# One step of a hybrid decoder layer on one core: the sample's queries are stored eight times for the spread loads, and the planned order comes from another list

## The chip, the cores and the metric

The kernel runs on one core of one Trainium2 chip. The metric is the device time of one execution in microseconds; less is better. A core has five instruction queues, one for each engine: TensorE (PE, matmuls and transposes), VectorE (DVE), ScalarE (ACT), GpSimd (POOL) and SyncE (SP), which in this kernel issues every DMA. Each engine runs its queue in order, and engines wait for each other by semaphores. Sixteen DMA engines do the transfers.

## What is computed

One step of one layer for a prompt of 2048 tokens and for a sample of 8 sequences with 8 new tokens each. Every token row is normed and projected, then goes through two mixers: dilated sliding-window attention with 8 heads of 64, and gated linear attention (GLA) with 4 heads. Both are gated and projected back. In outline, from the reference:

```
h = rmsnorm(x, norm_w)
z = h @ w_in
q, k, v, qb, kb, vb, g_lr, gate_a, gate_b = split(z)
q = rope(rmsnorm(heads(q, 8), q_norm_w), pos)
k = rope(rmsnorm(heads(k, 8), k_norm_w), pos)
o_a = mixture over (window, dilation) in ((128, 1), (512, 4), (2048, 16)) of softmax attention
o_b = rmsnorm(gla_chunked(qb / 8, kb, vb, log_sigmoid(g_lr @ w_gate_up + b_gate) / 16, s0))
y = x + concat(o_a * silu(gate_a), o_b * silu(gate_b)) @ w_out
```

For the sample, the keys and values of the last 2048 positions come from a cache in HBM, and each new token attends to 129 cached or new positions in each of the three branches.

## The kernel before

The prompt has 16 tiles of 128 tokens; the sample is one tile of 64 rows, the tile "s". Weights are split into two f16 parts, activations too, so that a projection of a prompt tile to 512 columns is 24 matmuls (L1748). In the order of time the kernel projects v, q and k of all tiles, runs the attention of branches 1 and 2 beside it (`unit`, with `attend`), then branch 3 beside the projections for GLA, then GLA, the gate of mixer B (`gb`), and last the output projection (L2111, `finish`), beside which the rest of the sample's attention is done.

The sample's attention against the cache is in two parts. For branches 2 and 3 each query needs its own set of 128 cached keys, so no matmul is used. `sample_scores(b, t)` handles the token t of sequence b, 64 calls in all: it loads the query's row, 512 f32 numbers, into all 128 partitions (tile `qb`, L1613, called the spread load here), loads 128 keys of the dilation 16 (`k3`, L1615), for t below 4 also 128 keys of the dilation 4 (`k2`, L1618), multiplies on POOL (`dot`, L1603) and sums over the head's 64 columns on DVE (L1604) into `sck`. After the eight tokens of a sequence `sck` goes to `sc_d` in HBM. The tiles `qb` and `k3` have two buffers each, `k2` and the product `pr` have one. `sample_pair` reads `sc_d` much later (`Sc`), beside the output projection.

The queries come from `q_d`, a scratch array in HBM. Before, it has 2048 + 64 rows of 512, of which the last 64 are written and read: `qk_store` writes the sample's tile with one DMA (L1425), the 64 spread loads read a row each, and `sample_new` reads all 64 rows once more in the last stage (L2257).

Ahead of the output projection stand, for each tile, the gate (`so_gb`, `sa_gb` and `gw`, L1297 to L1389), the mix of the three branches (`combine`, L2141 to L2166: weights `w` from the branch's denominators, three products `tc`, their sum, and `mix`), its two f16 parts (`mt`, L2066 and L2067) and their transposes (`tm`, L2076). The output weights are scaled and split on ACT and DVE (`w_o`, L1278 and L1279).

The order of the instructions is not that of the program. The class `Plan` reads the traced program, gives each instruction a cost and each DMA a cost of the queue and a delay of landing (`price`), and lists which instructions depend on which. `settle` then runs a planner (`order`, a list scheduler with one queue for each engine and one for all DMAs, and `backward`) for some rounds to get a priority for each instruction, moves the priorities by a list of steps, and runs `order` once more; `fix` makes the outcome the order of each engine. In `price`, a load whose source's first step is 0 (one row to all partitions) has 3.16 times the cost that its bytes would have, other loads in short rows 1.11 times. Before, a step is a seed: `moved` draws from it an instruction, a kind of group (the instructions that write the same tile; the one instruction; those of its engine within a reach) and an amount.

Of the kernel before, what the change touches and what calls it, by code (L numbers as in the profile page):

```python
# [18 lines left out]
P = 128  # L19
# [4 lines left out]
S = 2048  # L24
NT = S // P
NS = 64
EPS = 1e-6
BIG = 3.0e38
LEVELS = [1, 2, 4, 8, 16, 32, 64]
# [22 lines left out]
class Plan:  # L52
# [581 lines left out]
                released(x)  # L634
        return place

    def moved(self, seed):

        import random

        r = random.Random(seed)
        n, kind = r.randrange(self.real), r.random()
        by = r.gauss(0, 1) * r.choice((1e3, 3e3, 1e4, 3e4))
        if kind < 0.5:
            return self.mates[self.leaf[n]], by
        if kind < 0.6:
            return [n], by
        reach, own = r.choice((1e4, 3e4, 1e5)), self.stem[n]
        return [
            x for x in range(self.real)  # L650
            if self.eng[x] == self.eng[n] and abs(self.base[x] - self.base[n]) < reach
            and (kind > 0.85 or self.stem[x] == own)
        ], by

    def settle(self, rounds, land, traffic, cross, bias, steps):

        self.rank()
        self.lands = {n: x + land for n, x in self.lands.items()}
        self.late = [
            x * (traffic if self.eng[n] == "SP" else 1.0) for n, x in enumerate(self.late)  # L660
        ]
        self.cross = cross
        prio = [-f for f in self.rank()]
        for _ in range(rounds):
            self.order(prio, bias)
            prio = [-x for x in self.backward(self.start)]
        self.leaf = [next((t for t, w, m in reversed(a) if w), "?") for a in self.acc]
        self.stem = [t.rstrip("_0123456789") for t in self.leaf]
        self.mates, self.base = {}, list(prio)
        for n, t in enumerate(self.leaf):  # L670
            self.mates.setdefault(t, []).append(n)
        for seed in steps:
            some, by = self.moved(seed)
            for x in some:
                prio[x] += by
        return self.order(prio, bias)[1]

# [13 lines left out]
def tile_hymba(ctx: ExitStack, tc: tile.TileContext, A: dict):  # L691
    nc = tc.nc
    PE, ACT, DVE, POOL, SP = nc.tensor, nc.scalar, nc.vector, nc.gpsimd, nc.sync
# [5 lines left out]
    def scratch(name, rows, cols):  # L699
        return dram.tile([rows, cols], F32, name=name)  # L700

    RT = S + NS
    q_d = scratch("q_d", RT, 512)
    k_d = scratch("k_d", RT, 512)
    v_d = scratch("v_d", RT, 512)
    zqk_d = scratch("zqk_d", RT, 512)
# [8 lines left out]
    sc_d = scratch("sc_d", 8 * P, 128)  # L715
    oa_d = scratch("oa_d", 2 * NS, 256)
    h_d = dram.tile([NT * P, 2 * KT * P], F16, name="h_d")
# [251 lines left out]
    with ExitStack() as c1:  # L969
# [114 lines left out]
        def fetch(t):  # L1084
            n = NS if t == "s" else P
            if t in (0, 1, 2, 3):
# [332 lines left out]
        def qk_store(nm_, o, n, t, rows):  # L1419
            if nm_ == "k":  # L1420
                SP.dma_start(kn_s if t == "s" else kw_p[rows, :], o[:n])
            if t == "s":
                if nm_ == "q":
                    ACT.activation(o[:n], o[:n], AF.Copy, scale=unq[:n])
                SP.dma_start((q_d if nm_ == "q" else k_d)[rows, :], o[:n])  # L1425
                return
            p_ = xp.tile([P, NH, 2, HD], F16, name=f"{nm_}p_{t}", tag=f"{nm_}p", bufs=1)
            src = o.rearrange("p (h d) -> p h d", h=NH)
            h, l = p_[:, :, 0], p_[:, :, 1]
            if nm_ == "k":  # L1430
                ACT.activation(h, src, AF.Copy, scale=scl["k"][:])
                DVE.scalar_tensor_tensor(l, src, scl["k"][:], h, ALU.mult, ALU.subtract)
            else:
                ACT.activation(h, src, AF.Copy)
                DVE.tensor_tensor(l, src, h, ALU.subtract)
            SP.dma_start(
                (qp_d if nm_ == "q" else kp_d)[rows, :], p_[:].rearrange("p h a d -> p (h a d)")
            )
# [156 lines left out]
            ]  # L1595


        q_s = q_d[S : S + NS, :]
        sk_state = {}

        def dot(out, kt, qt, tag):
# [6 lines left out]
        def sample_scores(b, t):  # L1608
# [1 line left out]
                sk_state["sc"] = sk.tile([P, 2, 64], F32, name=f"sck_{b}", tag="sc")  # L1610
            sc = sk_state["sc"]
            qt = sk.tile([P, 512], F32, name=f"qb_{b}_{t}", tag="qbc")
            SP.dma_start(qt[:], q_s[8 * b + t : 8 * b + t + 1, :].to_broadcast([P, 512]))  # L1613
            k3 = sk.tile([P, 512], F32, name=f"k3_{b}_{t}", tag="k3")
            SP.dma_start(k3[:], ck[b].rearrange("(m r) c -> r m c", r=16)[t])  # L1615
            if t < 4:
# [258 lines left out]
        for i in range(3):  # L1875
            for lst, nm_ in ((st["qbd"], "qbd"), (Sbd, "Sbd"))[: 2 if i < 2 else 1]:
                t = gst.tile([P, 2, 256], F32, name=f"{nm_}{i}")
# [350 lines left out]
        for nh in range(2):  # L2228
            t = cb1.tile([P, NT + 1], F32, name=f"inv_o{nh}")
# [22 lines left out]
        QUADS = [(u, bb) for u in range(2) for bb in range(2)]  # L2252

        def sample_new():
            for nm_, src in (("q", q_d), ("k", k_d)):
                x = ssk.tile([NS, 512], F32, name=f"ls_{nm_}", tag="k1")
                SP.dma_start(x[:], src[S : S + NS, :])  # L2257
                pt = ps_P.tile([P, 512], F32, name=f"ts_{nm_}", tag="PT")
                for p in range(4):
                    PE.transpose(  # L2260
# [160 lines left out]
        weave(out, [sample_attention(), 4 * 9])  # L2421

    steps = (
# [33 lines left out]
    )  # L2457
    plan = Plan(tc, nc)
    plan.fix(plan.settle(7, 600.0, 1.15, 60.0, 10.0, steps))


# [92 lines left out]
```

## Time and profile before

| what | value |
|---|---|
| three runs | 1267.63, 1264.02, 1263.77 us; median 1264.02 |
| the profiled execution | 1262.71 us |
| its span, first to last instruction | 1260.9 us |
| mean granted TensorE clock | 0.994 |
| DMA packets, bytes | 235832, 283.08 MB, mean 225 GB/s |

The profile is one execution taken by the hardware profiler. Its page has the busy time of each engine, the same in 40 slices, the chain of work that ended last, and the costliest groups of instructions. The trace behind it can be asked for stretches of time, waits, single tiles and instructions in order of time. In a row of a stretch stand its length, the busy time of each engine with the number of instructions, the granted TensorE clock, the busy share of the 16 DMA engines, and the rate. In a row of a wait stand who waited, for whom, the total, how often, and the longest. In a row of the order of time stand start, length, engine, line, operation, tiles, and in brackets how long the engine had been idle. A row of a tile's view has the least, the median and the longest duration in ns, and the first and the last start.

### The profile page before, as it was taken

To read this page: it belongs to the slowest core of one execution; us is meant where nothing else is said; L and a number is where in the kernel's file an instruction comes from. 1 tells how busy PE (TensorE), PEld (TensorE's weight loads), DVE (VectorE), ACT (ScalarE), POOL (GpSimd) and SP (SyncE) were. 2 spreads that over 40 slices of the span, in tenths; PEclk is the share of its full clock that TensorE was granted. 3 is DMA by queue.
4 is the path that set the end of the run, shared out by engine and by line. 5 is a ranking of instruction groups with operands and counts; after the bars stand their busy time and mean duration, and the time that the engine had idled before them with its cause. 6 is when DMAs were issued, how large, how long until landed. Compare 5 with 4: busy or idle time off the path is not lost.

```text
span 1260.9 us, 26211 instructions
## 1 busy us (share of the span) xinstructions
PE 1202.4 (95%) x8942; PEld 723.7 (57%) x8942; DVE 956.1 (76%) x2450; ACT 817.8 (65%) x2191; POOL 549.0 (44%) x475
## 2 busy tenths in 40 slices
PE   5999999999999999998999999999999969999998
PEld 2444465667566566766677656665666435445443
DVE  7987887999889777777877557788888795269562
ACT  6654697889599888968778424678878632123220
POOL 0155433665755244643444766646533162024230
PEclk9999999999999999999999999999999979999999
DMA  8579935876945898699997867564435689988842
GB/s 291 187 213 270 258 126 138 233 200 188 231 153 148 232 251 301 183 272 273 265 272 231 242 184 195 172 209 137 139 135 193 217 299 343 381 333 326 323 169 68
DMA packets 235832, 283.08 MB, mean 225 GB/s; under 512 B 116193, under 2 KB 146866, under 8 KB 232626
## 3 DMA queue, kind: packets, MB, share of 16 engines
q1 hardware_dynamic: 235698, 281.40, 73.7%
q8 instruction: 71, 1.16, 0.4%
q14 instruction: 63, 0.52, 0.1%
HBM read 183.02 MB, written 75.24 MB: 205 GB/s over the span
## 4 chain that ended last, share of the span: by engine, by line
PE 53%; ACT 15%; DVE 15%; DMA 8%; issue 6%; SPq 2%; POOL 2%; DVEq 0%; ACTq 0%; POOLq 0%
PE Y L2111 13%; PE acc_v L1748 5%; PE acc_qkb L1748 4%; PE acc_k L1748 4%; PE acc_q L1748 3%; PE acc_vb L1748 3%; PE t L1046 3%; ACT p L1039 3%; PE O L1061 3%; PE s L1028 3%; PE acc_g L1748 3%; DMA o_d<-o 2%; PE OS L2360 2%; DMA qb<-q_d 2%; DVE p L1036 2%
## 5 line engine op out<-in xcount | busy, mean ns | idle before, releaser
L1748 PEld LDWEIGHTS <-hr 128*128 128x128 f16 x1824 | 172.0, 98 | 112.8 <-issue 13.2
L1603 POOL TENSOR_TENSOR pr<-k,qb 128x512 f32<-128x512 f32 x128 | 168.2, 1314 | 148.2 <-DVE sck L1604 73.9
L1039 ACT ACTIVATE p<-p,o 128x256 f32<-128x256 f32 (+1 forms) x384 | 173.7, 458 | 24.7 <-DVE o L1036 24.2
L1748 PEld LDWEIGHTS <-hl 128*128 128x128 f16 x1248 | 120.0, 98 | 119.5 <-issue 5.6
L2111 PE MATMUL Y<-w_o,mh 128*128 128x512 f16 x768 | 178.5, 383 | 2.4 <-ACT mh L2077 1.3
L1013 POOL TENSOR_TENSOR pt<-p,pt 128x512 f16<-128x512 f32 (+1 forms) x80 | 91.4, 1142 | 147.2 <-ACT pt L1012 124.1
L1061 PE MATMUL O<-v,pt 128*128 128x128 f16 x1200 | 135.6, 219 | 5.4 <-DVE pt L1009 1.9
L1046 PE MATMUL t<-ident,p 128*128 128x128 f32 x600 | 123.5, 278 | 4.7 <-ACT p L1039 3.0
L2111 PEld LDWEIGHTS <-mh 128*128 128x128 f16 x768 | 73.5, 99 | 89.5 <-issue 7.7
L1604 DVE TENSOR_REDUCE sck<-pr 128x8 f32<-128x512 f32 x128 | 86.9, 679 | 45.6 <-POOL pr L1603 45.2
L1061 PEld LDWEIGHTS <-pt 128*128 128x128 f16 x1200 | 93.7, 98 | 37.9 <-DVE pt L1009 4.6
L1748 PE MATMUL acc_g<-w_g,hr 128*128 128x256 f16 (+1 forms) x768 | 112.0, 276 | 0.0
L1748 PE MATMUL acc_v<-w_v,hl 128*128 128x512 f16 x384 | 108.5, 383 | 0.4 <-ACT zs_q L1323 0.4
L1748 PE MATMUL acc_k<-w_k,hl 128*128 128x512 f16 x384 | 104.4, 379 | 0.5 <-DVE vp L1410 0.4
L1748 PE MATMUL acc_vb<-w_vb,hr 128*128 128x512 f16 x384 | 100.9, 379 | 3.9 <-DVE so_g L1297 3.4
L1748 PE MATMUL acc_q<-w_q,hl 128*128 128x512 f16 x384 | 102.4, 379 | 0.1
L2159 POOL TENSOR_TENSOR tc<-oc,w 128x512 f32<-128x512 f32 x32 | 43.9, 1390 | 125.1 <-DVE w L2151 97.7
L1036 DVE CUSTOM_DVE_ANT_0 p<-s,m3w,scl_s 128x128 f32<-128x128 f32 (+1 forms) x256 | 87.7, 394 | 12.1 <-PE s L1028 4.7
L1748 PE MATMUL acc_gb<-w_gb,hr 128*128 128x512 f16 x384 | 94.8, 380 | 0.0
L1028 PE MATMUL s<-kk,qq 128*128 128x256 f16 (+1 forms) x512 | 87.7, 264 | 4.8 <-DVE o L1036 2.9
L1046 PEld LDWEIGHTS t<-ident,p 128*128 128x128 f32 x600 | 74.6, 141 | 26.8 <-ACT p L1039 11.5
L1748 PE MATMUL acc_qkb<-w_qkb,hr 128*128 128x512 f16 x288 | 81.0, 379 | 0.0
(528 smaller groups left out, 2532.4 us busy)
## 6 DMA issues: line engine op xcount, KB each, us to landing
k<-in_cache_k_win SPq DMA_DIRECT2D x104, 256.0 KB
sv_b<-in_cache_v_win SPq DMA_DIRECT2D x24, 1024.0 KB
hr<-h_d SPq DMA_DIRECT2D x44, 512.0 KB
qb<-q_d SPq DMA_DIRECT2D x64, 256.0 KB
oc<-o_d SPq DMA_DIRECT2D x48, 264.0 KB
o_d<-o SPq DMA_DIRECT2D x64, 132.0 KB
x<-in_x_prompt SPq DMA_DIRECT2D x16, 512.0 KB
h_d<-hl SPq DMA_DIRECT2D x16, 512.0 KB
```

The lines of the kernel that those rows point to most:

```text
L1013: POOL.tensor_tensor(l, f, h, ALU.subtract)
L1028: PE.matmul(s_ps[:, i * w : (i + 1) * w], q, k, start=(n == 0), stop=(n == len(prods) - 1),)
L1036: DVE.tensor_tensor_reduce(s[:, sl], s_ps[:, sl], mask, neg, BIG, ALU.add, ALU.min, nmf(i))
L1039: ACT.activation(s[:, sl], s[:, sl], AF.Exp, bias=nmf(i), scale=-1.0, accum_out=denf(i))
L1046: PE.transpose(p_ps[:, i * P : (i + 1) * P], t["s"][:, i * P : (i + 1) * P], ident[:])
L1061: PE.matmul(o_, t["pt"][:, c, (i * nb + b) * P : (i * nb + b + 1) * P], vf(i, b), start=(n == 0), stop=(n == 2 * nb - 1),)
L1603: POOL.tensor_tensor(pr[:], kt, qt, ALU.mult)
L1604: DVE.tensor_reduce(out, pr[:].rearrange("p (u k d) -> p u k d", u=2, k=4), AX.X, ALU.add)
L1748: PE.matmul(z, a_[:, k, :], w[:, p_, k, cols], start=(k == 0 and i == 0), stop=(k == KT - 1 and i == 2),)
L2111: PE.matmul(Y[:], a_[:, k, :], w_[:, part, k, :512], start=(i == 0), stop=(i == len(prods) - 1),)
L2159: eng.tensor_tensor(t_[:], oc[:, g, :, 0:64], w[:, g].unsqueeze(2).to_broadcast([P, NH, HD]), ALU.mult,)
L2360: PE.matmul(OS[32 * x : 32 * x + 32, 0:256], ps(x), vs_[bb][:, 256 * u : 256 * u + 256], start=(i == 0), stop=(i == 13),)
```

## The change

The queries' array gets 64 x 8 rows, eight copies of each row one after the other. The store writes all eight from the same 64 rows of SBUF; each spread load reads each of the eight copies for 16 partitions. The last stage's load reads the first copy of each. The steps are written out as kind, instruction and amount, there are others, and `settle` runs 8 rounds in place of 7 and adds 800 ns in place of 600 to the landing of every DMA.

```
+COPIES = 8
...
-    def moved(self, seed):
-
-        import random
-
-        r = random.Random(seed)
-        n, kind = r.randrange(self.real), r.random()
-        by = r.gauss(0, 1) * r.choice((1e3, 3e3, 1e4, 3e4))
-        if kind < 0.5:
-            return self.mates[self.leaf[n]], by
-        if kind < 0.6:
-            return [n], by
-        reach, own = r.choice((1e4, 3e4, 1e5)), self.stem[n]
+    def some(self, kind, n):
+
+        if kind == 0:
+            return self.mates[self.leaf[n]]
+        if kind == 1:
+            return [n]
+        reach, own = (1e4, 3e4, 1e5)[(kind - 2) % 3], self.stem[n]
         return [
             x for x in range(self.real)
             if self.eng[x] == self.eng[n] and abs(self.base[x] - self.base[n]) < reach
-            and (kind > 0.85 or self.stem[x] == own)
-        ], by
+            and (kind > 4 or self.stem[x] == own)
+        ]
...
-        for seed in steps:
-            some, by = self.moved(seed)
-            for x in some:
+        for kind, n, by in steps:
+            for x in self.some(kind, n):
                 prio[x] += by
...
-    q_d = scratch("q_d", RT, 512)
+    q_d = scratch("q_d", NS * COPIES, 512)
...
-                SP.dma_start((q_d if nm_ == "q" else k_d)[rows, :], o[:n])
+                if nm_ == "q":
+                    SP.dma_start(
+                        q_d[:].rearrange("(n c) d -> n c d", c=COPIES),
+                        o[:n].unsqueeze(1).to_broadcast([n, COPIES, 512]),
+                    )
+                else:
+                    SP.dma_start(k_d[rows, :], o[:n])
...
-        q_s = q_d[S : S + NS, :]
+        q_s = q_d[:].rearrange("(n c) d -> n c d", c=COPIES)
...
-            SP.dma_start(qt[:], q_s[8 * b + t : 8 * b + t + 1, :].to_broadcast([P, 512]))
+            SP.dma_start(
+                qt[:],
+                q_s[8 * b + t].unsqueeze(1).to_broadcast([COPIES, P // COPIES, 512]),
+            )
...
-            for nm_, src in (("q", q_d), ("k", k_d)):
+            for nm_, src in (("q", q_s[:, 0]), ("k", k_d[S : S + NS, :])):
...
-                SP.dma_start(x[:], src[S : S + NS, :])
+                SP.dma_start(x[:], src)
...
-        798993397, 379503271, 976436735, 990016090, 697217584, 129675417, 778155539, 369111627,
...
+        "0:5458:-16991 0:8969:5952 0:11965:-616 0:11088:-1869 7:2138:107148 7:9297:746 1:7616:-38203 "
...
     plan = Plan(tc, nc)
-    plan.fix(plan.settle(7, 600.0, 1.15, 60.0, 10.0, steps))
+    steps = [tuple(int(v) for v in s.split(":")) for s in steps.split()]
+    plan.fix(plan.settle(8, 800.0, 1.15, 60.0, 10.0, steps))
```

More of the change, by code (lines that the diff above doesn't have):

```diff
@@ L2423, in tile_hymba @@
     steps = (
[33 rows of a table removed]
+        "0:5458:-16991 0:8969:5952 0:11965:-616 0:11088:-1869 7:2138:107148 7:9297:746 1:7616:-38203 "
+        "0:12947:-45966 0:7858:-1202 0:8993:-9721 0:11207:1338 0:12414:-22948 0:2785:568 2:7882:482 "
+        "0:13191:-5777 7:6456:-1801 0:12039:-25583 2:9671:-3071 1:11970:2684 0:4079:888 0:12511:2211 "
+        "7:12806:14319 2:11088:-1131 1:9455:-1166 5:12533:6158 4:12072:1006 6:13107:-12916 "
+        "0:11421:939 2:12512:-2659 0:2694:-1278 0:884:-2650 0:11699:386 2:9371:-19361 7:9595:1411 "
@@ new lines, in tile_hymba @@
+        "0:8180:-1634 0:131:-33360 0:8335:2230 0:12574:17330 4:10740:36294 5:13053:-18482 0:11314:901 "
+        "0:12770:-57727 2:11754:-11651 2:83:-486 2:9738:-4054 0:9859:241 0:11520:-6852 1:4550:1125 "
+        "1:9450:4209 0:9810:-2191 0:1483:6184 0:7604:1065 0:11926:1473 0:2969:-803 0:11902:-13373 "
+        "0:9869:858 0:7799:1184 1:7323:-2242 0:11862:1010 2:7599:-1710 4:12890:-3990 0:3314:-321 "
+        "0:12858:-8458 2:8318:-306 0:12663:4711 0:11696:-28466 2:585:-12871 0:8547:-1650 0:218:-9747 "
@@ new lines, in tile_hymba @@
+        "2:306:1162 0:9812:-905 0:1481:-6600 2:11787:-17923 3:6854:-3170 2:11722:-1723 4:12826:838 "
+        "2:12889:5890 0:899:-21570 0:7896:-561 1:11705:-2302 3:7529:7552 0:6417:4380 7:2206:-26301 "
+        "1:7162:5565 0:11471:-14242 0:3515:-11904 1:6180:44502 2:10377:-4666 3:11734:4677 "
+        "0:9868:-1426 1:11970:5175 1:11229:20463 1:7981:-17456 2:9866:-30366 0:378:-6896 0:6718:2094 "
+        "7:6902:-2089 0:7585:-609 0:2207:1158 0:525:-4127 2:9899:-558 7:786:4231 0:7586:-2526 "
+        "2:7513:-4967 0:11285:-13958 0:7787:-937 1:6366:-19740 0:1586:41436 0:1615:67579 5:3279:2149 "
@@ new lines, in tile_hymba @@
+        "0:379:1817 6:4462:40619 0:2201:-5171 2:6348:1053 0:241:-3536 0:13009:1074 0:12538:3262 "
+        "0:2736:37184 0:381:-43808 1:11671:8551 0:7858:-833 0:6920:1155 1:7978:-2435 0:7993:-2215 "
+        "1:5558:2497 1:11326:15648 2:12660:-717 0:11302:-10962 0:8105:-836 0:10105:-953 0:9504:-299 "
+        "1:11670:940 0:5789:-9618 1:11669:1909 4:11437:649 0:2358:854 7:9066:693 3:5184:374 "
+        "2:744:48087 0:10238:1946 0:10310:374 4:12692:-23810 0:51:9899 0:508:3283 0:6464:-21540 "
+        "0:7631:1226 0:1424:-1027 0:5802:15538 0:9549:5173 2:12393:-9781 1:11970:-16132 0:1403:-505 "
@@ new lines, in tile_hymba @@
+        "0:12379:-11939 3:1129:-2029 0:7619:675 0:11480:2957 0:5664:2549 5:11735:-5359 0:1154:2543 "
+        "0:7856:-2622 0:10113:-2606 0:11314:2388 2:11331:-1411 0:8237:1745 0:106:-1903 1:5949:-47755 "
+        "0:11088:-5649 2:9434:-106 0:8634:-837 0:11813:-14769 2:11440:4621 6:11698:1301 1:4346:12095 "
+        "1:1403:-833 0:4066:21998 2:11881:-4363 0:10457:12802 0:8696:-1234 2:11770:-573 0:10473:-1072 "
+        "4:12168:98 3:7910:-1308 0:6878:-17067 0:9515:2771 1:7604:5493 1:7796:458 2:10421:-2098 "
@@ new lines, in tile_hymba @@
+        "1:10106:-1941 1:7978:1857 0:4950:1192 2:2666:-533 0:11488:-1339 2:4909:-1150 0:5870:-16012 "
+        "1:9357:4749 0:11691:2011 0:11245:-441 1:6013:368 0:11784:-3241 0:6015:-339 0:7830:-6961 "
+        "0:11917:-47929 1:11669:-6995 0:8247:334 6:5697:-1816 0:1868:548 0:5976:-7782 0:8880:1002 "
+        "2:4984:-2620 6:10501:-2789 4:814:-28201 0:6023:-18290 1:6202:517 1:10453:777 1:8254:-11088 "
+        "0:10900:-1105 0:4971:1623 0:5061:305 0:12408:14180 7:9647:-3589 0:10601:787 5:7356:-4568 "
@@ L2457, in tile_hymba @@
+        "0:8377:-236 2:3601:2801 0:4032:2045 2:686:7775 0:11445:-744 1:11161:-913 0:6840:1497 "
+        "0:82:853 0:5039:-25177 0:4949:-2068 0:6192:-306 0:11285:-809 2:11305:-1120 0:4032:-472 "
+        "6:7293:4552 1:8416:-8020 0:3765:-54367 "
     )
     plan = Plan(tc, nc)
-    plan.fix(plan.settle(7, 600.0, 1.15, 60.0, 10.0, steps))
+    steps = [tuple(int(v) for v in s.split(":")) for s in steps.split()]
+    plan.fix(plan.settle(8, 800.0, 1.15, 60.0, 10.0, steps))
 _INS = [
```

32 rows, old and new, of the table steps are left out of this document.

## The prediction

> **What bounds the kernel now.** I read the page's engine totals first, then the busy times by stage, then TensorE's waits.
>
> ```profile
> span 1260.9 us, 26211 instructions
> PE 1202.4 (95%) x8942; PEld 723.7 (57%) x8942; DVE 956.1 (76%) x2450; ACT 817.8 (65%) x2191; POOL 549.0 (44%) x475
> ```
>
> ```profile
> core 0: us, PE busy (x) PEld busy (x) DVE busy (x) ACT busy (x) POOL busy (x), PEclk, DMA share, GB/s
> 0.00:31.50 31.50, 16.50 (x100) 9.22 (x101) 22.62 (x56) 21.16 (x36) 0.40 (x6) 1.00 0.88 291
> ...
> 219.00:535.00 316.00, 309.62 (x2374) 206.12 (x2372) 263.11 (x698) 271.17 (x772) 172.24 (x133) 1.00 0.76 212
> 535.00:700.00 165.00, 158.17 (x1362) 112.60 (x1362) 124.47 (x442) 127.80 (x442) 69.46 (x59) 1.00 0.97 260
> 700.00:878.00 178.00, 173.54 (x1357) 109.43 (x1354) 129.49 (x280) 104.39 (x262) 111.25 (x109) 1.00 0.65 192
> ...
> 1007.50:1027.00 19.50, 9.54 (x47) 4.46 (x46) 19.07 (x38) 6.78 (x10) 12.34 (x8) 0.65 0.72 241
> ...
> 1229.00:1260.90 31.90, 27.24 (x133) 12.26 (x131) 6.59 (x10) 1.74 (x3) 0.00 (x0) 0.99 0.21 70
> ```
>
> TensorE is the bound: it is idle for 1260.9 - 1202.4 = 58.5 us in all. Of these, 15.0 lie at the start (31.50 - 16.50) and 4.7 at the end, where there is little to reorder. In the 659 us in which the spread loads run (219 to 878) it is idle for 6.4 + 6.8 + 4.5 = 17.7 us. One short stage, 1007.5 to 1027, holds 19.50 - 9.54 = 10.0 us of idle time, and its granted clock is 0.65 where the other stages show 1.00. There DVE is busy for 19.07 of 19.50 us. So the change can help the end only through those two places.
>
> ```profile
> 993.66 14.42 PE L1748 MATMUL acc_gb<-w_gb,hr 128*128 128x512 f16 x66
> 1016.92 1.03 PE L2076 MATMUL tm<-ident,mt 128*128 128x128 f16 x8 [8.84 <-ACT mt L2066]
> 1019.07 0.61 PE L2111 MATMUL Y<-w_o,mh 128*128 128x512 f16 x1 [1.12 <-ACT mh L2077]
> ...
> 1020.33 5.70 PE L2111 MATMUL Y<-w_o,mh 128*128 128x512 f16 x15
> ...
> 1027.18 0.61 PE L2076 MATMUL tm<-ident,mt 128*128 128x128 f16 x8
> ```
>
> This is the order of time on TensorE at that place. The last gate projections run at 14.42 / 66 = 0.218 us each, a matmul close behind a matmul. Then TensorE stands for 8.84 us until the first output tile is mixed, and for 1.12 more. After it 15 output matmuls take 5.70 us, where 15 x 0.218 = 3.3 would do, and eight turns take 1.03 where they later take 0.61: 2.4 + 0.4 us go to the lowered clock. The hole costs 8.84 + 1.12 + 2.8 = 12.8 us.
>
> **The change, part by part.** The diff has two independent parts: copies of the queries, and an order of all instructions that comes out of another list and other parameters.
>
> *The spread loads (64 of them).* No instruction is added or removed.
>
> ```profile
> L1603 POOL TENSOR_TENSOR pr<-k,qb x128: 1257/1273/2248, 225.6 to 877.8; 128x512 f32<-128x512 f32 x128
> L1613 SPq DMA_DIRECT2D qb<-q_d x64: 319/422/1490, 219.0 to 854.7; - x64
> ```
>
> ```profile
> L2281 POOL COPY Scg<-Sc x4: 397/400/855, 910.5 to 1137.2; 128x256 f32<-128x256 f32 x4
> ```
>
> ```profile
> POOL pr L1603 <- DMA qb<-q_d: 8.0, 5, 2.4
> ```
>
> ```profile
> 199.81 0.55 SPq L1505 DMA_DIRECT2D v<-vp_d  x1
> ```
>
> ```profile
> 835.38 0.32 SPq L1613 DMA_DIRECT2D qb<-q_d  x1
> ```
>
> ```profile
> 201.00:201.60 0.60, 0.60 (x5) 0.27 (x4) 0.57 (x2) 0.58 (x4) 0.51 (x1) 1.00 0.19 61
> ...
> 200.00:200.50 0.50, 0.50 (x8) 0.35 (x6) 0.50 (x5) 0.50 (x2) 0.00 (x0) 1.00 0.73 256
> 835.90:838.40 2.50, 1.68 (x17) 0.72 (x15) 1.74 (x4) 2.46 (x6) 0.64 (x1) 1.00 0.30 105
> 220.80:223.80 3.00, 3.00 (x18) 1.63 (x17) 2.35 (x4) 2.21 (x8) 3.00 (x3) 1.00 0.59 222
> ```
>
> The load issued at 835.38 has its stretch almost alone: 105 GB/s x 2.50 us is its 256 KB, and the 16 DMA engines are busy for 0.30 of it. The store at 200.0 moved 256 GB/s. So reading one 2 KB row 128 times is slow, and not because the engines are full: 0.30 x 16 x 2.50 us / 128 = 94 ns of engine time for a packet. Two such loads side by side, with other transfers, move 222 GB/s (220.80 to 223.80), at most 1.5 us each. Eight copies could bring a load to between 256 KB / 256 GB/s = 1.0 us and its present 1.5 to 2.5. But the new load's source is eight copies by sixteen repeats, so its outermost length is 8. The load at 199.81 has an outermost length of 4 (four rows to a residue), and while it runs, at 201.00, the engines are busy for 0.19 and move 61 GB/s. If the outermost length is the number of engines used, eight engines take 16 packets each: 16 x 94 ns = 1.5 us. I therefore take a gain of 0 to 1.5 us for each load, and 0.5 as nearest to the rows with two loads in flight.
>
> The Trainium skill (DMA: Bandwidth & Descriptors, Why a DMA increments its semaphore by 16 and not by 1) says that a load from this queue uses the largest number of engines up to 16 that divides the outermost lengths of both sides, here 8 of 8 and 128. By it a spread load would have half the engines; with all 16 the sum would have 0.8 us a load in place of 1.5. The row at 201.00 agrees with it.
>
> What hides the loads: their only reader is POOL's product, whose wait for them is 8.0 us in all, and the scores' first reader on POOL starts at 910.5, 31 us after the last product (877.8 + 1.3), their last at 1137.2. TensorE waits for none of it. So 64 x 0.5 = 32 us off the transfers are worth little: between -8.0 (all of POOL's wait reaches the end) and the loss of the first rival; I take **-1**. SP's issue may grow from 0.32 to the 0.55 of the four-row load, 64 x 0.23 = 15 us of SP over 636 us: hidden as long as SP's own waits for buffers last, since what follows a spread load on SP is mostly the key load of the same product.
>
> *The store.* It writes 1 MB in place of 128 KB.
>
> ```profile
> 214.61 0.48 SPq L1425 DMA_DIRECT2D q_d<-t_qk_s  x1
> ...
> 215.82 1.92 SPq L1116 DMA_TRANSPOSE hl<-ht  x1
> ...
> 219.04 0.87 SPq L1613 DMA_DIRECT2D qb<-q_d  x2
> ```
>
> At the rate of 200.00, 256 / 0.73 = 351 GB/s for full engines, 0.92 MB more take 2.6 us. Behind it in the queue are a transpose for a later projection and the first spread loads, which must wait for its landing; whatever SP has behind that wait (transposes for queries and keys) is as late. From 219 to 535 TensorE is idle only 6.4 of 316 us, and works on projections whose inputs are there. I take **0**, bounds 0 and +2.6. The later load of the sample's queries reads the first copies, as many bytes as before: 0.
>
> *The order.* Every engine's queue is set anew. The diff doesn't show the result, so only bounds and places can be had. The place with most to win is the hole. DVE's order ahead of it:
>
> ```profile
> 1001.45 0.17 DVE L2141 TENSOR_TENSOR mn<-oc 128x8 f32<-128x8 f32 x1
> 1001.53 0.75 DVE L1279 SCALAR_TENSOR_TENSOR w_o<-wr_o,ns_o,w_o 128x512 f16<-128x512 f32 x1
> ...
> 1002.51 0.74 DVE L1279 SCALAR_TENSOR_TENSOR w_o<-wr_o,ns_o,w_o 128x512 f16<-128x512 f32 x1
> 1003.17 0.68 DVE L1305 CUSTOM_DVE_ANT_0 so_gb<-so_gb,sa_gb 128x512 f32<-128x512 f32 x1
> ...
> 1003.89 0.74 DVE L1297 TENSOR_SCALAR so_gb<-acc_gb,wi_gb 128x512 f32<-128x512 f32 x1
> ...
> 1005.22 0.74 DVE L1279 SCALAR_TENSOR_TENSOR w_o<-wr_o,ns_o,w_o 128x512 f16<-128x512 f32 x1
> ...
> 1005.96 0.74 DVE L1279 SCALAR_TENSOR_TENSOR w_o<-wr_o,ns_o,w_o 128x512 f16<-128x512 f32 x1
> 1006.75 0.69 DVE L1305 CUSTOM_DVE_ANT_0 so_gb<-so_gb,sa_gb 128x512 f32<-128x512 f32 x1
> ...
> 1008.10 0.23 DVE L2151 SCALAR_TENSOR_TENSOR w<-w,smxa,mn 128x24 f32<-128x24 f32 x1
> ...
> 1013.38 1.78 DVE L1305 CUSTOM_DVE_ANT_0 so_gb<-so_gb,sa_gb 128x512 f32<-128x512 f32 x1
> ```
>
> The first tile's weights (L2141 to L2151) take from 1001.45 to 1008.33, and between their small steps stand output weights (L1279) and gates (L1297, L1305) of 0.75 + 0.74 + 0.68 + 0.74 + 0.74 + 0.74 + 0.69 = 5.1 us; at 1013.38 another gate takes 1.78 ahead of the mix. An order that puts the first tile first brings its mix forward by up to 5.1 + 1.8 = 6.9 us. TensorE's 8.84 would shrink to about 2, and with it perhaps the 2.8 of the lowered clock. A list made anew may as well leave the hole, or open another. I take **-7** of the 12.8, and **-2** of the 17.7 us of the loops, with bounds of -17.7 and, as one more hole of that kind, +12.8.
>
> The sum: -1 + 0 - 7 - 2 = -10. The profiled execution took 1262.7 us, 1.8 more than its span and 1.3 under the runs' median of 1264.0. 1262.7 - 10 = **1252.7, told as 1253**.
>
> **The rivals.**
> *Half the engines fill up (slower).* Between 535 and 700, 19 of the 64 spread loads are issued, and the DMA share is 0.97.
>
> ```profile
> L1613 SPq DMA_DIRECT2D qb<-q_d x19: 319/422/1490, 539.8 to 693.2; - x19
> ```
>
> If a load goes to eight engines, these take 8 packets more for each: 19 x 8 x 94 ns = 14.3 us in a stretch in which they have none to spare, and every other transfer ends with its slowest engine. For it: the 0.97 and the row at 201.00. Against it: the other eight engines and the stalls of the one row are relieved, and TensorE is idle only 6.8 us there, mostly for other reasons. It decides once those eight have no gap left. 1262.7 + 14.3 = **1277**. The rule named above is what would bring it about.
> *Another hole (slower).* The new order lets a stage's first tile come late behind work that has time, on DVE or in SP's queue behind the store: +12.8 for one hole as priced, **1275**. For it: one such hole is in an order made by the same planner. Against: nothing in the diff moves work there.
> *Nothing moves the end.* Loads hidden, hole as it is: **1262**. For it: 95% busy and POOL's 8.0.
> *Much more.* The hole closed, half of the loops' 17.7 and half of POOL's 8.0: 12.8 + 8.9 + 4.0 = 25.7, **1237**.
>
> **How the numbers follow.** A measurement tells apart about 0.3%, 3.8 us: faster is under 1260.2, slower over 1267.8. The forecast has a chance of 0.50 (its own range 1240 to 1261, with 0.04 of it within 0.3%), half the engines 0.15, another hole 0.15, nothing 0.12, much more 0.08. Faster: 0.46 + 0.08 = 0.54; within: 0.04 + 0.12 = 0.16; slower: 0.30. The range reaches from 1237 to 1277, the ends of the outer cases.
>
> **What would show it.** The stage with the last gate projections should show TensorE idle for about 3 us in place of 10.0, with a clock near 1.00; if it is still about 10, the -7 is wrong. A lone spread load should be over in 1.5 us or less at a share of about 0.5 or below; a share as for other loads means 16 engines, 2.5 us that copies don't help. POOL's wait for the spread loads should fall under 8.0 without TensorE's idle time in 535 to 700 following it; if that idle time grows by ten or more, the first rival holds. If TensorE's busy time itself moves by more than 5 us from 1202.4, the order acts through TensorE's own queue, which no step here prices.

## The result, and the profile after

The changed kernel takes 1292.18 us (median of 6 runs, 1289.66 to 1297.14) against 1263.95 us before (6 runs, 1261.94 to 1267.63): ratio 1.0227, 95% interval 1.0201 to 1.0253. It is 28.2 us slower; the forecast was 10 us faster. The page of the changed kernel, span and engine totals:

```profile
span 1288.0 us, 26217 instructions
PE 1207.6 (94%) x8942; PEld 724.9 (56%) x8942; DVE 951.8 (74%) x2450; ACT 818.7 (64%) x2191; POOL 542.6 (42%) x475
```

TensorE has the same 8942 matmuls. Its idle time grew from 58.5 to 1288.0 - 1207.6 = 80.4 us, and its busy time by 5.2 us at a mean clock of 0.991 (0.994 before): together the 27.1 us by which the span grew. The stretches of the changed kernel, with the columns of the table of before:

```profile
core 0: us, PE busy (x) PEld busy (x) DVE busy (x) ACT busy (x) POOL busy (x), PEclk, DMA share, GB/s
...
219.00:535.00 316.00, 301.01 (x2256) 197.94 (x2255) 251.36 (x662) 257.84 (x725) 163.13 (x126) 0.99 0.79 212
535.00:700.00 165.00, 146.37 (x1226) 101.83 (x1225) 115.35 (x393) 115.86 (x392) 68.14 (x55) 0.98 0.98 238
700.00:878.00 178.00, 170.39 (x1323) 110.41 (x1321) 120.03 (x286) 100.35 (x274) 107.52 (x105) 0.99 0.69 200
...
1007.50:1027.00 19.50, 19.20 (x95) 9.66 (x94) 9.91 (x28) 13.70 (x34) 4.21 (x4) 1.00 0.62 192
1027.00:1229.00 202.00, 195.33 (x1499) 96.94 (x1498) 139.14 (x306) 61.15 (x97) 66.80 (x48) 0.98 0.92 341
```

In the 659 us of the spread loads TensorE is idle for 15.0 + 18.6 + 7.6 = 41.2 us, where it was 17.7. The stretch that held the hole is full, 19.20 of 19.50 us; but the stretches are fixed in time and the kernel is slower, so it holds earlier work now. TensorE's longest waits of the whole execution (who waited, for whom, total, times, longest) name what is new:

```profile
PE mx_v L1192 <- DVE w_v L1249: 14.8, 1, 14.8
PE acc_vb L1752 <- DVE so_g L1292: 10.8, 4, 6.3
PE t L1041 <- ACT p L1034: 8.7, 11, 1.6
PE s L1023 <- DMA kk<-kp_d: 6.9, 4, 3.6
...
PE tm L2080 <- ACT mt L2070: 3.2, 1, 3.2
```

The first row is the start of the kernel, which costs no more than before: TensorE is idle for 14.9 of the first 31.5 us, 15.0 before. The last row is the old hole: it stands in the order of time at 1042 now, and is 3.2 us long where it was 8.84. The three between are, but for 1.1 us, in the loops. The spread loads themselves, in the view of POOL's product and its loads:

```profile
L1614 SPq DMA_DIRECT2D qb<-q_d x64: 586/610/1450, 231.7 to 833.9; - x64
...
  DMA qb<-q_d: 14.7, 7
```

SP holds a spread load for 610 ns in the median (422 before), and POOL waits 14.7 us for them by this view (8.0 before). TensorE's longest wait in the loops, the 6.3 us for `so_g`, shows how lateness gets there. Order of time on TensorE, and the waits of all engines, both from 590 to 606 of the changed kernel:

```profile
595.51 2.78 PE L1752 MATMUL acc_g<-w_g,hr 128*128 128x256 f16 x24
604.58 1.87 PE L1752 MATMUL acc_vb<-w_vb,hr 128*128 128x512 f16 x4 [6.29 <-DVE so_g L1292]
```

```profile
PE acc_vb L1752 <- DVE so_g L1292: 6.3, 1, 6.3
...
ACT vbs_s L1392 <- DMA ga_d<-so_g0s: 3.7, 1, 3.7
ACT jw_gb L1242 <- DMA wr_gb<-in_w_in: 3.6, 1, 3.6
...
DVE so_g L1292 <- DMA ga_d<-so_g1s: 2.9, 1, 2.9
```

TensorE stands behind a gate on DVE, and DVE stands for the last 2.9 us ahead of that gate on the landing of a store (`ga_d`) that has nothing to do with the sample's queries. ACT stands on two more such DMAs (`ga_d`, `wr_gb`). (The view of all engines also has POOL's product wait 6.1 us for `ga_d`. By the semaphore events that is a false name: the product starts at 601.19, just after DVE's sum `sck` ended at 601.1, while `ga_d` lands at 603.95.) Two edits were made at once, so this view can't say which of them is to blame.

### The profile page after: what moved, and what is told of

It is laid out like the page before. It is cut to its first block, busy times and chain, and to the rows that moved or that the text cites. A ratio compares the mean times of both kernels' runs of the same rounds, so it can differ in the third digit from the quotient of the medians.

```text
span 1288.0 us, 26217 instructions
## 1 busy us (share of the span) xinstructions
PE 1207.6 (94%) x8942; PEld 724.9 (56%) x8942; DVE 951.8 (74%) x2450; ACT 818.7 (64%) x2191; POOL 542.6 (42%) x475
## 5 line engine op out<-in xcount | busy, mean ns | idle before, releaser
L1604 POOL TENSOR_TENSOR pr<-k,qb 128x512 f32<-128x512 f32 x128 | 164.2, 1283 | 174.6 <-DVE sck L1605 107.2
L1041 PE MATMUL t<-ident,p 128*128 128x128 f32 x600 | 126.2, 280 | 9.7 <-ACT p L1034 8.7
L1056 PEld LDWEIGHTS <-pt 128*128 128x128 f16 x1200 | 95.8, 99 | 41.2 <-POOL pt L1008 4.6
L1752 PE MATMUL acc_q<-w_q,hl 128*128 128x512 f16 x384 | 108.6, 384 | 3.3 <-ACT zs_k L1318 3.0
L1752 PE MATMUL acc_k<-w_k,hl 128*128 128x512 f16 x384 | 109.9, 379 | 0.7 <-DVE w_k L1274 0.5
L1023 PE MATMUL s<-kk,qq 128*128 128x256 f16 (+1 forms) x512 | 85.7, 266 | 11.7 <-DMA kk<-kp_d 6.9
L1752 PE MATMUL acc_gb<-w_gb,hr 128*128 128x512 f16 x384 | 91.3, 380 | 0.0
```

The lines of the kernel that those rows point to most:

```text
L1023: PE.matmul(s_ps[:, i * w : (i + 1) * w], q, k, start=(n == 0), stop=(n == len(prods) - 1),)
L1041: PE.transpose(p_ps[:, i * P : (i + 1) * P], t["s"][:, i * P : (i + 1) * P], ident[:])
L1056: PE.matmul(o_, t["pt"][:, c, (i * nb + b) * P : (i * nb + b + 1) * P], vf(i, b), start=(n == 0), stop=(n == 2 * nb - 1),)
L1604: POOL.tensor_tensor(pr[:], kt, qt, ALU.mult)
L1752: PE.matmul(z, a_[:, k, :], w[:, p_, k, cols], start=(k == 0 and i == 0), stop=(k == KT - 1 and i == 2),)
```

## The experiments

In every kernel below that keeps an order, the planner's price for the spread loads and the store is held at that of the kernel whose order it is, so that each engine has the very same sequence of instructions and only the DMA named differs.

**Loads and order apart.** Old order with the copies as in the change; new order with one row and the small store; and both orders with eight copies turned inside out, so that the outermost length of the source is 16:

```
 e1, and after:  q_s[8 * b + t].unsqueeze(1).to_broadcast([COPIES, P // COPIES, 512])
 e3 and e4:      q_s[8 * b + t].unsqueeze(0).to_broadcast([P // COPIES, COPIES, 512])
 e2:             q_s[8 * b + t : 8 * b + t + 1, :].to_broadcast([P, 512])
```

> The order of every engine is that of before, instruction for instruction; only the store and the 64 spread loads have the changed kernel's form. If the form of the loads costs the time (eight engines, a longer issue on SP): 1280 to 1295 us. If the new order costs it: 1258 to 1268 us, and my forecast's own term for the loads alone was 1 us gained.

> The order of every engine is that of the changed kernel; the store and the spread loads have the form of before (one row). If the form costs the time: 1258 to 1270 us. If the order costs it: 1285 to 1295 us. If each costs a part, this and the run with the old order lie between, and their excesses over before add up to about 28 us.

> Order of before, eight copies, but a spread load's source has the sixteen repeats outermost and the eight copies inside, so that its outermost length is 16. If eight engines are what a load of the changed form suffers from, a load here lands about 1 us sooner than in the run with the outer copies, and the run takes no longer than before (1258 to 1266 us). If copies or the longer issue are the cost whatever the engines: as slow as the run with the outer copies.

> Order of the changed kernel, copies inside (outermost length 16). If eight engines cost the time: 1258 to 1270 us. If the order costs it: 1283 to 1295 us, whatever the loads look like.

| | median us | ratio to before (95%) | against before (1262.81) |
|---|---|---|---|
| e1, old order, copies outermost | 1272.18 | 1.0081 (1.0049 to 1.0113) | +9.4 |
| e2, new order, one row | 1272.89 | 1.0086 (1.0067 to 1.0106) | +10.1 |
| e3, old order, copies inside | 1261.91 | 0.9995 (0.9977 to 1.0014) | -0.9 |
| e4, new order, copies inside | 1271.34 | 1.0073 (1.0051 to 1.0094) | +8.5 |

Both edits cost, and more together (28.2) than apart (9.4 + 10.1 = 19.5, where e2's expectation had about 28). e1 and e4 lie between the two ranges that were named for them, since neither edit is the whole cause. The loads' part is not the copies, the store of 1 MB or a longer issue as such, since e3 has all three (a spread load holds SP for 540 ns in the median, 602 in e1): the same copies, each read sixteen times, with the two lengths of the source exchanged, cost nothing that can be told from noise. The exchange also changes the order in which the copies are read; e6 below leaves that out. A nearly lone spread load in before, e1 and e3 (length of the stretch, busy times, clock, DMA share, GB/s):

```profile
836.00:838.40 2.40, 1.58 (x17) 0.72 (x15) 1.64 (x4) 2.36 (x6) 0.64 (x1) 1.00 0.31 109
```

```profile
846.00:848.20 2.20, 1.38 (x16) 0.63 (x15) 1.45 (x3) 2.20 (x5) 0.00 (x0) 1.00 0.35 119
```

```profile
838.50:840.00 1.50, 0.68 (x8) 0.18 (x8) 0.74 (x2) 1.50 (x4) 0.02 (x1) 1.00 0.68 175
```

Each moves the load's 256 KB. In e1 the share stays under one half; in e3 it is 0.68, and the load is over in 1.5 us in place of 2.4. So copies did help this lone load, with the outermost length 16. It brings the kernel nothing: nobody but POOL's product waits for it.

**A dose of engines.** Old order: four copies outermost; one row, no copies and the small store, but its 128 readings written as 8 by 16; sixteen copies outermost.

```
 e5:  COPIES = 4
 e6:  q_s[8 * b + t : 8 * b + t + 1, :].to_broadcast([8, 512]).unsqueeze(1).to_broadcast([8, P // 8, 512])
 e9:  COPIES = 16
```

> Order of before, four copies with the copies outermost: by the theory that the outermost length is the number of DMA engines, four engines take 32 packets of 94 ns each, 3.0 us a load, and the run's excess over before grows well beyond the 9 us of the eight copies: 1280 to 1310 us. If the cost came with the number of copies stored, or with the longer issue on SP, it would be the 9 us or less: 1264 to 1273 us.

> Order and store of before, no copies: a spread load still reads one row 128 times, but written as eight times sixteen, so that its outermost length is 8. By the theory of the engines this alone costs what the eight copies cost, 1269 to 1282 us. If the copies in HBM (their store, their addresses) cost it, this is as before: 1260 to 1266 us.

> The order of before, sixteen copies of each query, the copies as the outermost length of both sides of the spread load (so sixteen packets-groups of 8 rows instead of 8 of 16). It stores 2 MB instead of 128 KB. Theory A (the loss of the loads is the number of DMA engines that the outermost length leaves them): no loss, ratio 0.998 to 1.002, and the landing of a spread load as in e3, near 4.2 us in the median. Theory B (it is the copies as such when they stand outermost, that is the scattered reading or the larger store): a loss at least as large as e1's, ratio 1.008 or more.

e5 1300.88 us, ratio 1.0299 (1.0268 to 1.033), +36.5; e6 1278.78 us, 1.0117 (1.0085 to 1.0149), +14.4; e9 1269.36 us, 1.0056 (1.004 to 1.0072), +6.1. The trace has each event by which a DMA raises its semaphore. Counted between 219 and 878, with the median time in us from the end of an issue to the last of them:

```
kernel                        events per spread load   spread load   k<-in_cache_k_win (dilation 16)   o_d<-o (L1520)
before, one row, 16                     16                4.54               3.92                          3.08
e3, 8 copies inside, 16                 16                4.17               3.72                          3.05
e9, 16 copies outermost                 16                4.06               3.49                          2.77
e1, 8 copies outermost                   9                4.98               4.12                          3.32
e6, one row as 8 x 16                    9                5.30               4.32                          3.48
e5, 4 copies outermost                   5                6.76               5.49                          4.24
e4, new order, 8 copies inside          16                4.25               3.85                          3.14
after, new order, 8 copies outermost     9                5.20               4.42                          3.77
```

The number of events follows the outermost length, 16, 8 or 4, with one more where it is below 16. By the Trainium skill (DMA: Bandwidth & Descriptors, Why a DMA increments its semaphore by 16 and not by 1) only the engines used raise the semaphore, and the issuing queue adds the rest at once; 9 and 5 events agree, for 8 and 4 engines. e6 reads the one row of before, in the same order and behind the same small store; only the outermost length differs, and it costs 14.4 us. Its issue is as long as e1's (602 ns), but e5 loses 36.5 us with an issue as short as e3's (537 ns), so the issue isn't the cost. Fewer engines delay not only the load: the two columns on the right are other transfers, of unchanged form, and they land later in the same order of kernels. That reaches the end by the chain of waits that ended last, whose shares by engine are, for before, e3, e1 and e5:

```profile
PE 53%; ACT 15%; DVE 15%; DMA 8%; issue 6%; SPq 2%; POOL 2%; DVEq 0%; ACTq 0%; POOLq 0%
```

```profile
PE 54%; DVE 16%; ACT 15%; DMA 7%; issue 4%; SPq 2%; POOL 1%; DVEq 0%; ACTq 0%; POOLq 0%
```

```profile
PE 48%; DVE 16%; ACT 15%; DMA 12%; issue 4%; SPq 3%; POOL 1%; DVEq 0%; ACTq 0%; POOLq 0%
```

```profile
PE 45%; DMA 16%; ACT 15%; DVE 14%; issue 5%; POOL 3%; SPq 3%; DVEq 0%; ACTq 0%; POOLq 0%
```

DMA is on that chain for 8, 7, 12 and 16%, and for 14% in e6. (In the changed kernel the chain can be followed back over the last 6% of the span only.) In e1 TensorE itself waits in 219 to 535, where it had waited 0.3 us for DMAs in all before:

```profile
PE s L1037 <- DMA kk<-kp_d: 2.0, 2, 1.5
PE O L1070 <- DMA v<-vp_d: 1.3, 1, 1.3
```

Neither of these is a spread load. At eight engines e1, with copies, is 5 us better than e6 without, but their intervals overlap, so that copies help the kernel is not shown.

e9 has 16 engines and the earliest landings, and still loses 6.1 us; its expectation of no loss failed. The place is the store, now 2 MB. Order of time on SP, POOL and TensorE in e9:

```profile
212.50 0.57 SPq L1435 DMA_DIRECT2D q_d<-t_qk_s  x1
213.12 0.67 SPq L1440 DMA_DIRECT2D k_d<-t_qk_s  x1
213.88 12.83 SPq L1125 DMA_TRANSPOSE hl<-ht  x1
```

```profile
226.05 2.46 POOL L1362 TENSOR_TENSOR t_qk<-zs_q,ct_qk 128x512 f32<-128x512 f32 x2 [6.28 <-DMA k_d<-t_qk_s]
228.47 0.67 POOL L1022 TENSOR_TENSOR pt<-p,pt 128x256 f16<-128x256 f32 x1
```

```profile
229.20 0.50 PE L1070 MATMUL O<-v,pt 128*128 128x128 f16 x3 [5.05 <-POOL pt L1022]
```

Two stores are in flight, and SP stands in the issue of the transpose behind them for 12.83 us. POOL waits 6.28 us until `k_d`, stored behind `q_d`, has left the tile, and TensorE 5.05 us for what POOL does next. With the store of 1 MB the same transpose in e3 holds SP for

```profile
214.51 7.55 SPq L1125 DMA_TRANSPOSE hl<-ht  x1
```

against 1.92 us before and 4.70 us in e5 (0.5 MB): 0.7 to 0.9 us for each copy more. At eight copies (e3) POOL waits only 1.0 us for `k_d`, and TensorE 1.2 us behind it:

```profile
PE O L1070 <- POOL pt L1022: 1.2, 1, 1.2
```

**Where the new order loses.** TensorE's idle time (length less busy time of each stretch; for the last column the page's span less its busy time):

| | 219 to 535 | 535 to 700 | 700 to 878 | 1007.5 to 1027 | 1027 to 1229 | whole span |
|---|---|---|---|---|---|---|
| before | 6.4 | 6.8 | 4.5 | 10.0 | 2.0 | 58.5 |
| e3, old order, 16 engines | 9.6 | 6.6 | 4.1 | 10.0 | 2.6 | 61.5 |
| e1, old order, 8 engines | 12.4 | 9.5 | 3.1 | 8.9 | 4.3 | 66.1 |
| e6, old order, one row, 8 engines | 9.9 | 11.7 | 7.9 | 2.4 | 11.3 | 70.5 |
| e2, new order, one row | 9.9 | 15.2 | 3.7 | 1.2 | 6.3 | 68.4 |
| e4, new order, 16 engines | 11.6 | 10.4 | 3.4 | 1.7 | 5.8 | 64.6 |
| after | 15.0 | 18.6 | 7.6 | 0.3 | 6.7 | 80.4 |

The stretches are fixed in time, and in a slower kernel the hole moves on into the next one: in e2 TensorE's wait for `mt` ends at 1029.0. So the last two stretches have to be read together. By e2's row they gain 8.8 - 4.3 = 4.5 us, the loops give back 3.5 + 8.4 - 0.8 = 11.1, and the rest of the 9.9 us is lost ahead of 219 (2.6) and in 878 to 1007.5 (0.7). In e4 the two other transfers of the table above land about as early as before (3.85 and 3.14 us), and it loses 8.5 us all the same: it is not by these that the new order loses. Two stretches of e2, and TensorE's waits in the first of them:

```profile
535.00:700.00 165.00, 149.76 (x1259) 104.89 (x1257) 117.01 (x405) 117.44 (x400) 71.56 (x57) 0.98 0.98 250
...
1007.50:1027.00 19.50, 18.34 (x85) 8.13 (x83) 19.29 (x47) 11.38 (x20) 7.79 (x6) 1.00 0.90 328
```

```profile
PE acc_vb L1751 <- DVE so_g L1300: 6.4, 3, 4.0
PE t L1049 <- ACT p L1042: 3.7, 5, 1.1
PE O L1064 <- ACT pt L1011: 2.4, 1, 2.4
```

The first stretch loses by several waits. The gate (first row) costs 6.4 us in all, the longest wait 4.0, where before had in the same stretch:

```profile
PE acc_vb L1748 <- DVE so_g L1297: 2.2, 2, 1.1
```

Hybrids with one row and the small store were to find the place. They take one order for all that its plan starts before a time, and the other behind it:

```
+    early = {x for x in range(old.real) if old.start[x] < cut}
+    old.fix({
+        e: [x for x in old_out[e] if x in early] + [x for x in new_out[e] if x not in early]
+        for e in old_out
+    })
```

> One row, as before. Every engine follows the old order for what the old plan starts before 560 us, then the changed kernel's order for the rest. If the new order loses its 10 us behind 560 us (TensorE idle there in 535 to 700 is 15 us in place of 7): 1268 to 1276 us. If it loses them ahead of 560 us: 1258 to 1266 us.

> One row, as before. The old order for what the old plan starts before 905 us, the changed kernel's order for the rest, the last stages. The new order has no hole at the end of the gate projections. If that is a gain that the earlier stages eat up: 1252 to 1261 us. If the last stages of the new order gain nothing: 1262 to 1270 us.

> One row as source and the small store. The order of before for all that its plan starts before 700 us, the new order from there on. The new order's loss lies between 560 and 905 us (e7 has 1.0095, e8 1.0004). Theory A (it is made by the stretch 560 to 700, where loads of the next heads, weights and spread loads meet): ratio 0.998 to 1.003. Theory B (it is made by 700 to 905, where the outputs of the second branch and the next stage's weights meet): ratio 1.007 to 1.011. In between: it is spread over both.

> One row as source and the small store. The new order for all that its plan starts before 560 us, the order of before from there on. Theory A (the new order loses only after 560 us): ratio 0.997 to 1.003. Theory B (the stretch before 560 us loses too, and what e7 shows is then a second cost): ratio above 1.004. A gain below 0.997 would say that the early part of the new order is worth keeping.

Old until 560, 905 and 700: 1275.88 us, 1.0095 (1.0073 to 1.0118); 1264.76 us, 1.0004 (0.9991 to 1.0017); 1276.02 us, 1.0111 (1.0092 to 1.0131). New until 560, then old (e7c): 1267.04 us, 1.003 (1.0018 to 1.0042). The first two seem to put the loss between 560 and 905, the third puts it behind 700; e8 gains nothing by the new last stages. But a seam can open a hole of its own. TensorE's waits of e7 in 535 to 700 and of e7b in 700 to 780, and a stretch of e8 (length, TensorE's busy time, clock, DMA share, GB/s), have one each:

```profile
PE t L1070 <- ACT p L1063: 12.1, 7, 7.7
```

```profile
PE acc_vb L1772 <- DVE so_g L1321: 19.7, 2, 19.2
```

```profile
905.00:960.00 55.00, 45.73 (x412) 0.91 0.35 114
```

e7b's whole loss in its profiled execution is one wait of 19.2 us that neither parent has, and e8's 45.73 were 54.24 before. So e7, e7b and e8 settle nothing about the place. e7c has no such hole: with the new order up to 560 it loses 3.8 us, at the upper edge of the range that was to mean no loss there, but with an interval that excludes 1.

**The late part alone.** Six more seams, later.

> One row as source, small store; the order of before for all that its plan starts before 860 us, the new one behind it. Theory A (the late part of the new order is a gain by itself: TensorE's hole at the gate's end is closed and nothing is paid for it but what the seam costs): TensorE busy 960 to 1027 near 64 (55.25 before), ratio 0.993 to 0.997 if the seam costs under 1 us, and 1.0 when it costs 8 as in e8. Theory B (the closed hole opens again behind it, whatever the seam): ratio 1.0 or more with no hole at the seam.

> As e10, the seam at 930 us. Theory A: TensorE busy 960 to 1027 above 60 and no hole of over 3 us at 905 to 960: ratio 0.993 to 0.997. Theory B: 1.0 or more with no hole at the seam.

> As e10, the seam at 955 us. Theory A: ratio 0.993 to 0.997 if the steps that close the hole (the gate's products brought forward among the attention's outputs) still come early enough; with them cut off the hole stays and the ratio is 0.999 to 1.001. Theory B: 1.0 or more with the hole closed.

> As e10, the seam at 980 us, about 27 us ahead of the hole of before. Theory A and B alike: the gate's products stand where before has them, so the hole stays (TensorE busy 960 to 1027 near 55) and the ratio is 0.998 to 1.002. It is the control: a ratio above 1.003 would say that the tail of the new order, behind 1027 us, costs by itself.

> One row as source, small store; the order of before for all that its plan starts before 970 us, the new one behind it. Theory A (the new order's part behind the attention closes half of the hole at the gate's end, and nothing is paid for it where the seam opens no other): ratio 0.995 to 0.999, TensorE busy 1007.5 to 1027 near 14 to 15 (before 9.54). Theory B (e13 was the luck of one seam): 1.000 to 1.004 as in e11 and e12.

> As e14, the seam at 990 us. Theory A: ratio 0.995 to 1.000, less of the hole closed than in e13 if the products that fill it stand before the seam. Theory B: 1.000 to 1.004.

| old order until | median us | ratio to before (95%) | TensorE idle 960 to 1007.5 (before 1.8) | 1007.5 to 1027 (before 10.0) |
|---|---|---|---|---|
| 860 (e10) | 1267.12 | 1.0036 (1.0016 to 1.0056) | 0.7 | 4.1 |
| 930 (e11) | 1265.78 | 1.0018 (1.0004 to 1.0032) | 2.7 | 4.3 |
| 955 (e12) | 1266.68 | 1.0036 (1.0023 to 1.0049) | 9.1 | 3.8 |
| 970 (e14) | 1264.44 | 1.0004 (0.9992 to 1.0016) | 6.7 | 4.1 |
| 980 (e13) | 1258.99 | 0.9979 (0.9961 to 0.9997) | 3.9 | 5.2 |
| 990 (e15) | 1259.03 | 0.9968 (0.9956 to 0.9979) | 2.5 | 7.4 |

In e10 and e11 the seam's hole is ahead of 960 (e10: TensorE busy 35.41 of 45 us in 860 to 905, 43.66 before; e11: 46.24 of 55 in 905 to 960, 54.24 before); in e12 and e14 it is in 960 to 1007.5. None of these four gains, though a gain was named as possible for each; e14, between e12 and e13, came out where "the luck of one seam" had been named. e13 was expected to be a control without effect, and that was wrong: what shortens the hole stands behind the seam at 980. TensorE's order of time at the hole, e13 and e15:

```profile
1014.48 1.03 PE L2100 MATMUL tm<-ident,mt 128*128 128x128 f16 x8 [4.37 <-ACT mt L2090]
```

```profile
1015.50 1.04 PE L2100 MATMUL tm<-ident,mt 128*128 128x128 f16 x8 [6.61 <-ACT mt L2090]
```

The first output tile starts at 1014.48 and 1015.50 (1016.92 before). The two are 4.4 and 4.5 us under the kernel before of their own batch, and both intervals exclude 1; the best ratio here is e15's, with the old order up to 990 and the new one behind it, one row and the small store. They are two of six seams, and the gain is small. In their traces its smaller part is idle time (58.5 before, 57.4 in e13, 57.1 in e15) and its larger part busy time (1202.4, 1199.1, 1200.4), at a granted clock that is 0.50 for 6.8 us around the hole where it was so for 13.7 us. The stretches of before and e13 (length, TensorE's busy time, clock):

```profile
1011.30:1025.00 13.70, 6.96 (x28) 3.21 (x29) 13.67 (x28) 5.05 (x8) 9.85 (x6) 0.50 0.67 223
```

```profile
1013.20:1020.00 6.80, 4.71 (x23) 2.45 (x24) 6.73 (x14) 4.88 (x7) 5.13 (x3) 0.50 0.42 146
```

## Why the prediction was wrong

*The spread loads, -1: the step that failed.* They cost 9.4 us in the old order (e1). The prediction said that TensorE waits for none of it, and looked for the load's price only where its own reader waits. The runs showed the price elsewhere: with the load on half the engines other transfers land later (from e3 to e1 the key loads by 0.40 us in the median, `o_d` by 0.27), and TensorE, DVE and ACT wait for such transfers. Its bounds of -8.0 to +14.3 did hold e1's value; the value taken had the wrong sign. The lone load was to be over in 1.5 us or less at a share of about one half or below: in e1 it took 2.2 us at 0.35.

*The first rival* named the cause (8 engines; the row at 201.00 agreed), with a chance of 0.15. Its 14.3 us were worked out for 535 to 700, since only there the engines have no gap. e6 shows the eight engines without the large store: TensorE's idle time grows by 4.9 us there, but also by 3.5 in 219 to 535, at a mean share of 0.77, and by 3.4 in 700 to 878, at 0.68. (e1's row has 6.0 more in 219 to 535, but e3's, with 16 engines, has 3.2 more too.) It doesn't need a stretch whose mean share is near one; "it decides once those eight have no gap left" was wrong for the stretch as a whole.

*The store, 0.* Right in its cost (e3, which stores 1 MB, -0.9), wrong in its size: 2.6 us more were worked out, while the transpose behind it held SP 5.6 us longer, and TensorE waited 1.2 us in that trace.

*The hole, -7.* Right in kind, somewhat too large: TensorE's wait fell by 5.6 us, from 8.84 to 3.2, and in e2 the idle time of 1007.5 to 1229 by 4.5. The clock's part became smaller but did not go: in the changed kernel the granted clock is 0.50 for 6.8 us, from 1046.6 on, in place of 13.7.

*The loops, -2: the second step that failed.* With the loads as before they lose 3.5 + 8.4 - 0.8 = 11.1 us of TensorE's time (e2), within the +12.8 of "another hole" in size, but it is not one hole: it is many small waits, the longest 4.0 us. In sum the new order costs 10.1 where it was forecast to gain 9. Which of its steps bring those waits about stays open.

*The sum.* -1 and -9 were added as if independent. 28.2 - 19.5 = 8.7 us come only with both: e4 against after (1271.34, 1292.18) has the loads cost about 20 in the new order, against 9.4 to 10.3 in the old one. Two things in the traces fit this. From 16 to 8 engines the two other transfers of the table land 0.40 and 0.27 us later in the old order (e3 to e1), and 0.57 and 0.63 us later in the new one (e4 to after). And TensorE's longest wait for the gate `so_g` is 1.1 us before, 3.0 in e4 and 6.3 after. That the new order has less slack for late transfers is thus likely, but no run shows it by itself.

*The signs named in advance.* Two were ambiguous. Idle time in 535 to 700 grew by 11.8, which was to mean the first rival; e2 has 8.4 of it with one row. TensorE's busy time moved by 5.2, which was to mean that the order acts through its queue; e5 has 13.2 more with the old queue at a mean clock of 0.985, and e2 has 0.2 less with the new queue at 0.996, so this sign told of the granted clock and not of the queue. POOL's wait for the loads, to fall below 8.0, rose to 14.7 in the view.

## What to carry to other kernels

Before a load's source is reshaped, read its outermost length: here 16, 8 and 4 gave 16, 8 and 4 engines, and a load that TensorE never waits for still delayed other transfers that it does wait for; the exchange of two lengths in a source (e1 and e3) decided 10 us. A new order of a full kernel is worth what it gains in each stage less what it loses in the others: the last part of this one alone is a gain of 0.2 to 0.3% in two hybrids (e13, e15), the whole a loss of 0.9% (e2). A hybrid of two orders proves a place only after its seam has been looked at, and a stretch that is fixed in time holds other work once the kernel is slower.

## What the runs showed that was not expected

- 64 loads of 256 KB on 8 and on 4 of the 16 engines made the kernel 9.4 (e1) or 14.4 (e6) and 36.5 us (e5) longer, though TensorE never waits for them.
- A store from SBUF written many times over held up the transpose behind it in its queue, which took SP 1.92, 4.70, 7.55 and 12.83 us behind 1, 4, 8 and 16 copies of 128 KB (before, e5, e3, e9).
- A nearly lone load of one row read 128 times moved 109 GB/s at a share of 0.31; one of eight copies (e3), on 16 engines too, 175 GB/s at 0.68. The source of a load, not only the engines, set its speed.
- The hole cost in the granted clock as well: it was 0.50 for 13.7 us at the hole of 8.84 us, and for 6.8 us behind the one of 3.2 us that is left in the changed kernel. The first eight turns behind the hole took 1.03 us before and 0.62 us after.
